# A hybrid RWKV-7 / convolution / expert block: a fourth buffer for split weights, recurrence input begun four steps ahead, one small weight split per pass

## The chip, the cores and the metric

One core of one Trainium2 chip runs the whole program in one launch. The time is device microseconds of one execution; before and after are compared by medians of several runs, and the profile comes from one further execution.

## What is computed

A diffusion-backbone block over 2048 latent tokens and 256 context tokens of width 1024: a modulated RMS norm, one input projection, two branches beside each other (a bidirectional RWKV-7 recurrence over 8 heads of 64, and a gated convolution of width 3), an output projection, then 16 experts that each take their best 256 tokens. Cut to what the change touches:

```python
px = modulate(rmsnorm(x, norm1_g), sh1, sc1) @ w_in            # 1024 -> 1792 + 1536 columns
xr, xk, xv, xw, xa, xgl = split_rwkv(px_rw, shift_mu, grid_shift(px_rw))
def step(s, inp):                                              # the recurrence, both directions
    r_t, w_t, k_t, v_t, a_t, b_t = inp
    sa = einsum('bhvk,bhk->bhv', s, a_t)
    s = s * w_t[:, :, None, :] + sa[..., :, None] * b_t[:, :, None, :] + v_t[..., :, None] * k_t[:, :, None, :]
    return s, einsum('bhvk,bhk->bhv', s, r_t)
g = sigmoid(xgl) @ g_lora_up                                   # "second low-rank weights", 128 x 512
a_x = (groupnorm(y) * gn_g + gn_b + bonus) * g
x = x + g1 * (concat([a_x, short_conv(px_cv, conv_w)]) @ w_out)
out = rmsnorm(x + g2 * expert_choice_ffn(modulate(rmsnorm(x))), final_g)
```

## The kernel before, in words

Large products run in three matmuls instead of one: each operand is cut into a high piece (a cast to fp32r) and a low piece (the rest), and high·high, high·low and low·high are added up in PSUM. `split` (L127 to L134) makes the pieces of a weight: ScalarE casts (L129), then VectorE subtracts (L134). The tiles are `wH` and `wL`, in the pool `sh` that the first half of the program shares, three buffers each.

The program has four stages. First the conditioning (`ada_first`). Then the **projection** (`proj_phase`): four passes over 512 tokens each (pass 0 has the context too), and in each pass a loop over 14 column blocks. A block is `load_block` (two loads `wr` of 256 KB, two splits), then `block_mm` (L262), then an evacuation of PSUM into `e` by ScalarE, then the work on the block before, taken from `queue`: `post_wa`, `post_k` (blocks 1 to 4), `post_r` and `post_kd` (blocks 5 to 8, with the long VectorE scans `ct`, L508), `post_g` (block 9), `post_v` (blocks 10 to 13). `block_mm` goes through the tiles of 256 tokens one after the other, and in each through eight 128-row slices of the weights, the first four from the first half's pieces, the last four from the second half's:

```python
for (hH, hL), ps in zip(tiles, outs):
    for kt in range(KT):
        wH, wL = ws[kt // (KT // 2)]
        for wa, ha in ((wH, hH), (wH, hL), (wL, hH)):
            nc.tensor.matmul(ps, wa[:, kw, :], ha[:, kt, :], ...)
```

So for two tiles a block is 48 matmuls: 12 on the first half, 12 on the second, 12 on the first, 12 on the second. `gupH` and `gupL`, the pieces of the gate's low-rank weights (L324, L338), are made once, before the first pass, and stay.

Third is the **recurrence** (`wkv_phase`), 36 steps of 64 tokens, in both directions at once. For step s, `front(s)` makes masked products `g` (a tile with AHEAD = 5 buffers), `solve(n)` inverts triangles of the two steps 2n and 2n+1 on VectorE with 30 pairs of small instructions (L818, L820), after a trip of `g` through memory (`TI`) and before another one (`TO`), `merge(s)` reads `TO` back into `g` and begins with VectorE's transpose `tz` (L836), and `chain(s)` is the recurrence proper, which ends in the new state `Sb` (L886). `scale(n)` loads and scales the inputs of two steps. `begin(s)` is `front(s)`, and after odd s also `solve(s // 2)`. After `chain(s)` and `ready(s+1)` (the merge) come `scale((s+5) // 2)` if s is odd, `begin(s+5)`, and `fill`, which issues the convolution's products (`conv_gen`, again with `load_block`), the rest of the conditioning and the output projection as filler.

Fourth are the top-256 search and the experts (`moe_phase`, L1429 and L1446), with pools of their own.

The program text gives priorities; a scheduler sets the order of each engine's instructions from them, from the buffers and from its own timeline, and the engines then run that fixed order, each in order. The queue that issues nearly all loads and stores is SP's.

Of the kernel before, what the change touches and what calls it, by code (L numbers as in the profile page):

```python
# [7 lines left out]
F32 = mybir.dt.float32  # L8
# [12 lines left out]
KT = 8  # L21
# [115 lines left out]
def ada_first(ctx, tc, k, I, pool, psum, RH, RL, early):  # L137
# [18 lines left out]
    for kt in range(KT):  # L156
        if kt == 4:
            early(-2)
        for q in range(4):
            wH = k.bp.tile([128, 512], F32R, name="awH", tag="wH", bufs=3)  # L160
            wL = k.bp.tile([128, 512], F32R, name="awL", tag="wL", bufs=3)
            split(k, nc, wH, wL, w[kt][:, q * 512:q * 512 + 512], "act")
            nc.tensor.matmul(ps[q], sp[:, kt], wH, start=kt == 0, stop=False)
            nc.tensor.matmul(ps[q], sp[:, kt], wL, start=False, stop=kt == KT - 1)
# [76 lines left out]
def load_block(tc, k, I, b):  # L241
# [3 lines left out]
    for half in range(2):  # L245
        w = k.bp.tile([128, KT // 2, 128], F32, name="wr", bufs=2)
        nc.sync.dma_start(w, I["w_in"][b][:, half * KT // 2:(half + 1) * KT // 2])
        wH = k.bp.tile([128, KT // 2, 128], F32R, name="wH", bufs=3)
        wL = k.bp.tile([128, KT // 2, 128], F32R, name="wL", bufs=3)
        split(k, nc, wH, wL, w, "act")  # L250
        hs.append((wH, wL))
# [14 lines left out]
def proj_phase(ctx_, tc, k, I, S, fill):  # L266
    nc = tc.nc
    bp = k.bp
    with ExitStack() as ctx:
# [53 lines left out]
        up = pool.tile([128, 2, 2, 512], F32R, name="up", bufs=1)  # L323
        gupH = pool.tile([128, 512], F32R, name="gupH", bufs=1)  # L324
        gupL = pool.tile([128, 512], F32R, name="gupL", bufs=1)
        halo = pool.tile([128, 14, 2, PR], F32, name="halo", bufs=1)
        gn = pool.tile([128, 2, 512], F32, name="gn", bufs=1)

        def small():
            for q, nm in enumerate(("wup2", "aup2")):  # L330
# [4 lines left out]
                nc.vector.tensor_tensor(up[low, q], upr[low], up[low, q].bitcast(F32), op=OP.subtract)  # L335
            gupr = pool.tile([128, 512], F32, name="gupr", tag="sg", bufs=2)
            nc.sync.dma_start(gupr, I["gup"])
            split(k, nc, gupH, gupL, gupr, "act")  # L338
            nc.sync.dma_start(gn, _dap(I["gnrows"], 0, [[0, 128], [512, 2], [1, 512]]))
# [222 lines left out]

        def post_g(units, es):
            for u, e in zip(units, es):
                t0, n, _ = u
# [128 lines left out]
def wkv_phase(ctx_, tc, k, I, S, fill):  # L694
    nc = tc.nc
    with ExitStack() as ctx:
# [26 lines left out]
        NS = NCC + NCL  # L723
        AHEAD = 5
        k.y = {}
# [201 lines left out]
        begin(2)  # L927
        begin(3)
        scale(2)
        fill(1)  # L930
        begin(4)
        ready(0)
        for s in range(NS):
            chain(s)
            ready(s + 1)
            if s % 2:
                scale((s + 5) // 2)
            begin(s + AHEAD)
            fill(75 // 20 + 1 if s < TURN else 100, s >= TURN)
# [49 lines left out]
def conv_out_gen(tc, k, I, S):  # L989
# [5 lines left out]
    for i in OUT_ORDER:  # L995
# [4 lines left out]
        nc.sync.dma_start(cv, _dap(S["CV_"], r0, [[T, 128], [128 * T, 4], [1, 128]]))  # L1000
        aH = bp.tile([128, 4, 128], F32R, name="caH", tag="wH", bufs=3)
        aL = bp.tile([128, 4, 128], F32R, name="caL", tag="wL", bufs=3)
        split(k, nc, aH, aL, cv, "act")
# [9 lines left out]
def out_gen(tc, k, I, S):  # L1013
# [62 lines left out]
    def halves(j, x, y):  # L1076

        pt = turned(j, fl(y), 0)
        aH = bp.tile([128, 4, 128], F32R, name="oaH", tag="wH", bufs=3)
        aL = bp.tile([128, 4, 128], F32R, name="oaL", tag="wL", bufs=3)  # L1080
        split(k, nc, aH, aL, pt, "act")
# [8 lines left out]
    def square(x, ss):  # L1090
        junk = bp.tile([128, x.shape[-1]], BF, name="ojunk", tag="wL", bufs=3)
        nc.scalar.activation(junk, x, AF.Square, accum_out=ss)
# [8 lines left out]
    def flat(j, x, n):  # L1101
        pt = turned(j, x, 512 * n)
        tag = dict(tag="wH", bufs=3) if j < LAST else dict(tag="ev", bufs=5)
        z = bp.tile([128, 4, 128], F32, name="oxt", **tag)
# [553 lines left out]
```

## Time and profile before

| | us |
|---|---|
| median of 3 runs | 3159.18 (3146.18 to 3162.34) |
| the profiled execution | 3142.96 |
| its span, first to last instruction | 3141.1 |
| TensorE (PE) busy | 2881.8 (92%) |
| VectorE (DVE) busy | 2141.5 (68%) |
| ScalarE (ACT) busy | 1385.0 (44%) |
| GpSimd (POOL) busy | 667.4 (21%) |
| mean granted TensorE clock | 0.930 of full |

The conditioning lies in the span's first 50 us, the projection from there to about 626, the recurrence to about 1905, the search to about 1967, the experts to the end. A busy PE is one with matmuls in flight, at whatever clock; "granted clock" is 1.00 at 2.4 GHz and 0.50 at 1.2 GHz, and a mean between them is a mix of both in time. In a row on waits, the engine before the arrow stood idle until the instruction behind the arrow had ended.

### The profile page before, as it was taken

The page shows a single profiled execution, that of the slowest core. Times are in us where ns is not written, and L with a number is a line of the kernel's source. Part 1 is how long each engine was busy: PE and PEld are TensorE (multiplying, and loading weights), DVE is VectorE, ACT ScalarE, POOL GpSimd, SP SyncE. Part 2 cuts the span into 40 slices and gives each one's busy share as a digit, 9 for nine tenths or more (in the row PEclk, how much of TensorE's full clock was granted, in tenths as well). Part 3 has the DMA queues.
Part 4 walks back from the last instruction along what each step waited for, and adds up shares of the span by engine and source line. Part 5 has one row for each costly group of instructions (what it writes and reads, how often), then busy time and mean ns, then how long its engine had stood idle before and what let it go on. Part 6 is the DMA issues. An engine that isn't in the chain of part 4 may idle for free. (4 is left out here: it accounts for less than half of the span.)

```text
span 3141.1 us, 62585 instructions
## 1 busy us (share of the span) xinstructions
PE 2881.8 (92%) x24367; PEld 2612.9 (83%) x24367; DVE 2141.5 (68%) x4611; ACT 1385.0 (44%) x2279; POOL 667.4 (21%) x893
## 2 busy tenths in 40 slices
PE   6988989889999999999999994999999999999997
PEld 4877978878888888778888873998999899999886
DVE  7688687766666666667767646666666666666776
ACT  6556645423344443224445443444444444444453
POOL 0243242533333322112222121000000000000011
PEclk8989999977999999998788986999999999999998
DMA  6466555666666655766665551666666666666886
GB/s 248 144 201 193 178 175 170 201 170 152 154 169 165 173 141 162 204 176 169 164 151 143 124 165 47 201 219 205 188 204 204 195 197 208 207 203 206 267 285 228
DMA packets 408745, 577.43 MB, mean 184 GB/s; under 512 B 175864, under 2 KB 257912, under 8 KB 407424
## 3 DMA queue, kind: packets, MB, share of 16 engines
q1 hardware_dynamic: 397504, 533.58, 56.4%
q0 software_dynamic: 10656, 38.80, 5.3%
q8 instruction: 191, 3.13, 0.4%
q10 hardware_dynamic: 288, 1.05, 0.1%
q14 instruction: 106, 0.87, 0.1%
HBM read 444.73 MB, written 128.59 MB: 183 GB/s over the span
## 5 line engine op out<-in xcount | busy, mean ns | idle before, releaser
L129 ACT CAST wH<-wr 128x1024 fp32r<-128x1024 f32 (+1 forms) x592 | 528.9, 897 | 844.7 <-PE pg L1429 408.8
L134 DVE TENSOR_TENSOR wL<-wr,wH 128x1024 fp32r<-128x1024 f32 (+1 forms) x586 | 627.6, 1076 | 353.5 <-ACT wH L129 347.6
L1429 PE MATMUL pg<-xH,wH 128*128 128x256 f32 x2048 | 585.4, 286 | 15.8 <-ACT s L1433 15.8
L1429 PE MATMUL pg<-xL,wH 128*128 128x256 f32 x2048 | 576.2, 282 | 0.0
L1429 PE MATMUL pg<-xH,wL 128*128 128x256 f32 x2048 | 575.7, 281 | 0.0
L262 PE MATMUL pj<-hH,wH 128*128 128x256 f32 x1600 | 478.0, 299 | 25.5 <-ACT cu L671 7.4
L262 PE MATMUL pj<-hH,wL 128*128 128x256 f32 x1600 | 469.4, 294 | 23.6 <-DVE wL L134 22.6
L262 PE MATMUL pj<-hL,wH 128*128 128x256 f32 x1600 | 468.1, 293 | 1.4 <-DVE hL L134 1.1
L1429 PEld LDWEIGHTS pg<-xH,wH 128*128 128x128 f32 x2048 | 389.5, 190 | 17.9 <-ACT s L1433 16.5
L1429 PEld LDWEIGHTS pg<-xL,wH 128*128 128x128 f32 x2048 | 389.3, 190 | 1.5
L1429 PEld LDWEIGHTS pg<-xH,wL 128*128 128x128 f32 x2048 | 389.5, 190 | 0.0
L262 PEld LDWEIGHTS pj<-hH,wH 128*128 128x128 f32 x1600 | 318.4, 199 | 37.6 <-DVE cu L674 8.4
L262 PEld LDWEIGHTS pj<-hH,wL 128*128 128x128 f32 x1600 | 316.6, 198 | 30.9 <-DVE wL L134 28.9
L262 PEld LDWEIGHTS pj<-hL,wH 128*128 128x128 f32 x1600 | 318.5, 199 | 5.6 <-DVE hL L134 2.0
L1488 POOL DMA_INDIRECT ACC<-o,it x30 | 50.8, 1694 | 954.4 <-DVE o L1474 800.7
L1446 PE MATMUL pd<-wH,hL 128*128 128x512 f32 x512 | 201.9, 394 | 0.0
L1446 PE MATMUL pd<-wL,hH 128*128 128x512 f32 x512 | 201.9, 394 | 0.0
L1446 PE MATMUL pd<-wH,hH 128*128 128x512 f32 x512 | 199.9, 395 | 0.0
L818 DVE TENSOR_TENSOR x<-X,x 128x120 f32<-128x120 f32 (+12 forms) x540 | 157.8, 296 | 57.7 <-DMA X<-TI 46.0
L820 DVE TENSOR_TENSOR X<-X,x 128x120 f32<-128x120 f32 (+12 forms) x540 | 163.0, 305 | 12.3
L782 PE MATMUL pg<-ar,bk 64*128 64x128 f32 x1152 | 141.0, 323 | 17.1 <-DVE g L784 7.5
L782 PEld LDWEIGHTS pg<-ar,bk 64*128 64x128 f32 x1152 | 114.4, 215 | 33.7 <-issue 13.5
(428 smaller groups left out, 5456.9 us busy)
## 6 DMA issues: line engine op xcount, KB each, us to landing
wr<-in_w_gate_dram SPq DMA_DIRECT2D x128, 512.0 KB, 4.2
wr<-in_w_up_dram SPq DMA_DIRECT2D x128, 512.0 KB, 4.8
wr<-in_w_down_dram SPq DMA_DIRECT2D x128, 512.0 KB, 3.3
wr<-in_w_in_dram SPq DMA_DIRECT2D x208, 256.0 KB, 3.2
bk<-KBD SPq DMA_DIRECT2D x36, 512.0 KB, 5.6
ar<-NR SPq DMA_DIRECT2D x36, 512.0 KB, 5.9
adaw<-in_ada_b_dram SPq DMA_DIRECT2D x32, 512.0 KB, 3.7
inc<-C SPq DMA_DIRECT2D x36, 256.0 KB, 3.1
```

The costliest lines, as they stand in the source:

```text
L129: nc.scalar.copy(H_, src)
L134: (leng or nc.vector).tensor_tensor(L_, src, H_.bitcast(F32), op=OP.subtract)
L262: nc.tensor.matmul(ps, wa[:, kw, :], ha[:, kt, :], start=m == 0, stop=m == 3 * KT - 1)
L782: nc.tensor.matmul(pg[:, p], bk[rows, p], ar[rows, p], start=True, stop=True)
L818: nc.vector.tensor_tensor(tv, X[:, 0:r, t:t + 1].to_broadcast([128, r, m]), x[:, t:t + 1, t + 1:].to_broadcast([128, r, m]), op=OP.mult)
L820: nc.vector.tensor_tensor(X[:, 0:r, t + 1:], X[:, 0:r, t + 1:], tv, op=OP.add)
L1429: nc.tensor.matmul(ps, a[:, ws], b[:, kt], start=i == 0, stop=i == 23)
L1446: nc.tensor.matmul(po[2 * m + n], a[:, f, ms], b[:, ns], start=f == 0 and q == 0, stop=f == FB - 1 and q == 2)
L1488: nc.gpsimd.indirect_dma_start(out=S["ACC"], out_offset=bass.IndirectOffsetOnAxis(ap=ids[m][:, :1], axis=0), in_=o, in_offset=None, comput ...
```

## The change

Three edits. All tiles with the tags `wH` and `wL` get four buffers. `gupH` and `gupL` are no longer kept: `post_g` loads and splits the weights in each of the four passes, into a tile that shares the two buffers of `bk` (tag `kd`). In the recurrence AHEAD is 4 (four buffers of `g`), the prologue begins steps 0 to 3 instead of 0 to 4, and `begin(s + AHEAD)` stands before `scale`.

```diff
@@ ada_first, load_block, conv_out_gen, out_gen (all uses of the tags wH and wL)
-        wH = k.bp.tile([128, KT // 2, 128], F32R, name="wH", bufs=3)
-        wL = k.bp.tile([128, KT // 2, 128], F32R, name="wL", bufs=3)
+        wH = k.bp.tile([128, KT // 2, 128], F32R, name="wH", bufs=4)
+        wL = k.bp.tile([128, KT // 2, 128], F32R, name="wL", bufs=4)
@@ proj_phase
-        gupH = pool.tile([128, 512], F32R, name="gupH", bufs=1)
-        gupL = pool.tile([128, 512], F32R, name="gupL", bufs=1)
@@ small()
-            gupr = pool.tile([128, 512], F32, name="gupr", tag="sg", bufs=2)
-            nc.sync.dma_start(gupr, I["gup"])
-            split(k, nc, gupH, gupL, gupr, "act")
@@ post_g(units, es)
+            gupr = pool.tile([128, 512], F32, name="gupr", tag="sg", bufs=2)
+            nc.sync.dma_start(gupr, I["gup"])
+            gup = pool.tile([128, 2, 512], F32R, name="gup", tag="kd", bufs=2)
+            gupH, gupL = gup[:, 0], gup[:, 1]
+            split(k, nc, gupH, gupL, gupr, "act")
             for u, e in zip(units, es):
@@ wkv_phase
-        AHEAD = 5
+        AHEAD = 4
@@
         begin(2)
-        begin(3)
         scale(2)
         fill(1)
-        begin(4)
+        begin(3)
         ready(0)
         for s in range(NS):
             chain(s)
             ready(s + 1)
+            begin(s + AHEAD)
             if s % 2:
                 scale((s + 5) // 2)
-            begin(s + AHEAD)
             fill(75 // 20 + 1 if s < TURN else 100, s >= TURN)
```

Because the scheduler sets the order, instructions move in the first three stages on every engine; in the experts' stage TensorE's order is the same row for row. Two places matter below.

VectorE in the second pass, around blocks 7 and 8. `nrb<-e_3138` and `nrb<-e_3246` mix the results of blocks 7 and 8; `wL_3302` is the second half of block 9's pieces, `wL_3414` the first half of block 10's. Before:

```order
L425 SCALAR_TENSOR_TENSOR nrb_2741<-e_3138,cv_117,nrb_2741 128x8x64
L284 RECIPROCAL ssr_3817<-sss_3815 128x1
L285 TENSOR_SCALAR xt_3796<-xt_3796,ssr_3805 128x1024
L285 TENSOR_SCALAR xt_3808<-xt_3808,ssr_3817 128x1024
L508 SCALAR_TENSOR_TENSOR ct_3263<-rmask_423,sg_3261 128x512
L512 TENSOR_SCALAR bk_3164<-a_3175,cv_117,omka_421 128x8x64
L515 SCALAR_TENSOR_TENSOR bk_3164<-nrb_2741,a_3175 128x8x64
L425 SCALAR_TENSOR_TENSOR nrb_2741<-e_3246,cv_117,nrb_2741 128x8x64
L134 TENSOR_TENSOR wL_3302<-wr_3299,wH_3301 128x512
L508 SCALAR_TENSOR_TENSOR ct_3281<-rmask_423,sg_3279 128x512
L134 TENSOR_TENSOR wL_3414<-wr_3411,wH_3413 128x512
```

With the change (tile numbers are one lower: `e_3137` and `e_3245` are the same blocks' results, `wL_3413` and `wL_3419` the two halves of block 10):

```order
L420 SCALAR_TENSOR_TENSOR nrb_2740<-e_3137,cv_117,nrb_2740 128x8x64
L518 SCALAR_TENSOR_TENSOR kqb_2739<-kqb_2739,cv_117,nrb_2740 128x512
L507 TENSOR_SCALAR bk_3145<-a_3156,cv_117,omka_421 128x8x64
L510 SCALAR_TENSOR_TENSOR bk_3145<-nrb_2740,a_3156 128x8x64
L503 SCALAR_TENSOR_TENSOR ct_3172<-rmask_423,sg_3170 128x512
L134 TENSOR_TENSOR wL_3413<-wr_3410,wH_3412 128x512
L507 TENSOR_SCALAR bk_3163<-a_3174,cv_117,omka_421 128x8x64
L510 SCALAR_TENSOR_TENSOR bk_3163<-nrb_2740,a_3174 128x8x64
L134 TENSOR_TENSOR wL_3419<-wr_3416,wH_3418 128x512
L503 SCALAR_TENSOR_TENSOR ct_3262<-rmask_423,sg_3260 128x512
L420 SCALAR_TENSOR_TENSOR nrb_2740<-e_3245,cv_117,nrb_2740 128x8x64
```

By the mix of block 8 the low pieces of block 10 are now both made; before, the second half of block 9 was still to come.

VectorE in the recurrence, from the last instruction of a solve (here the one of steps 18 and 19) to the transpose that begins the merge of its first step. Before:

```order
L820 TENSOR_TENSOR X_14284<-X_14284,x_14283 128x15
L784 TENSOR_TENSOR g_15022<-pg_15023,mask0_7113 128x512
L1008 TENSOR_TENSOR cx_14427<-pj_14435,cx_14427 128x512
L766 TENSOR_TENSOR bk_15423<-bk_15423,ep_15428 128x8x64
L784 TENSOR_TENSOR g_15022<-pg_15024,mask0_7113 128x512
L784 TENSOR_TENSOR g_15022<-pg_15035,mask1_7119 128x512
L1008 TENSOR_TENSOR cx_14427<-pj_14449,cx_14427 128x512
L134 TENSOR_TENSOR caL_14762<-ccv_14759,caH_14761 128x512
L784 TENSOR_TENSOR g_15022<-pg_15036,mask1_7119 128x512
L766 TENSOR_TENSOR ar_15424<-ar_15424,em_15427 128x8x64
L836 STREAM_TRANSPOSE tz_15365<-g_13900 32x512
```

With the change:

```order
L820 TENSOR_TENSOR X_14600<-X_14600,x_14599 128x15
L766 TENSOR_TENSOR at_15467<-ar_15456,ep_15460 128x512
L1007 TENSOR_TENSOR cx_14381<-pj_14403,cx_14381 128x512
L134 TENSOR_TENSOR caL_14823<-ccv_14820,caH_14822 128x512
L836 STREAM_TRANSPOSE tz_15282<-g_14243 32x512
```

Over the 18 solves, at most six rows stand between the two in 2 of 18 before, and in 15 of 18 with the change. The transpose needs the trip of the solved triangles through `TO`.

## Rows read from the trace of the kernel before

**Rows 1.** Busy time by stretch; its length, engine busy (instructions), granted clock, DMA share, GB/s

```profile
core 0: us, PE busy (x) PEld busy (x) DVE busy (x) ACT busy (x) POOL busy (x), PEclk, DMA share, GB/s
265.00:315.00 50.00, 39.44 (x255) 35.56 (x254) 49.69 (x58) 34.33 (x59) 27.16 (x25) 0.89 0.74 229
315.00:400.00 85.00, 81.09 (x614) 75.31 (x613) 59.77 (x92) 53.25 (x94) 24.86 (x42) 0.98 0.50 165
400.00:445.00 45.00, 34.03 (x224) 31.05 (x224) 43.79 (x47) 16.87 (x28) 31.23 (x25) 0.91 0.72 221
1250.00:1850.00 600.00, 582.36 (x5901) 495.51 (x5900) 394.08 (x1251) 239.44 (x465) 118.57 (x161) 0.91 0.62 158
```

**Rows 2.** TensorE's waits from 50 to 626: us, times, longest

```profile
PE pj L262 <- DVE wL L134: 22.6, 18, 3.6
PE pj L262 <- ACT wH L129: 3.2, 5, 1.4
PE pw L577 <- DVE gt L585: 4.1, 1, 4.1
```

**Rows 3.** TensorE's waits from 265 to 315, then from 400 to 445

```profile
PE pj L262 <- DVE wL L134: 8.2, 3, 3.6
...
PE pj L262 <- DVE wL L134: 8.5, 5, 3.2
```

**Rows 4.** Timeline around 424 to 428: start, us, instruction, [idle before <-what ended it]

```profile
423.84 0.28 PE L262 MATMUL pj<-hH,wH 128*128 128x256 f32 x1
423.96 0.28 PE L262 MATMUL pj<-hL,wH 128*128 128x256 f32 x1
...
425.28 1.59 POOL L514 TENSOR_TENSOR bk<-kqb,bk 128x512 f32<-128x512 f32 x1 [0.42 <-POOL kqb L525]
...
425.67 1.75 DVE L134 TENSOR_TENSOR wL<-wr,wH 128x512 fp32r<-128x512 f32 x1
...
427.47 0.58 PE L262 MATMUL pj<-hH,wL 128*128 128x256 f32 x1 [3.24 <-DVE wL L134]
```

**Rows 5.** The low pieces' subtractions and the casts, 50 to 626 (min/median/max; busy, mean ns)

```profile
L134 DVE TENSOR_TENSOR wL<-wr,wH x123: 659/692/1804, 70.3 to 625.1; 128x512 fp32r<-128x512 f32 x123
...
L129 ACT CAST wH<-wr 128x512 fp32r<-128x512 f32 x124 | 75.6, 617 | 111.2 <-PE pj L262 53.6 <-DMA wr<-in_w_in_dram 53.5 <-PE pc L262 3.8
```

**Rows 6.** The one split of the gate's weights: duration min/median/max, start

```profile
L134 DVE TENSOR_TENSOR gupL<-gupr,gupH x1: 684/684/684, 36.8 to 36.8; 128x512 fp32r<-128x512 f32 x1
```

**Rows 7.** DMA issues of the recurrence: count, KB each, median us to landing

```profile
TO<-X SPq DMA_DIRECT2D x36, 128.0 KB, 3.2
g<-TO SPq DMA_DIRECT2D x72, 64.0 KB, 3.7
```

**Rows 8.** Waits in the recurrence: of VectorE, of ScalarE, of TensorE

```profile
DVE tz L836 <- DMA g<-TO: 13.5, 6, 3.4
...
ACT wH L129 <- PE pj L262: 117.5, 46, 7.5
...
PE pu L869 <- ACT w L863: 12.4, 6, 4.6
```

**Rows 9.** VectorE's timeline, 1613 to 1736: two states, and one solve with its merge

```profile
1614.81 0.85 DVE L886 TENSOR_TENSOR Sb<-sc,pc 64x256 f32<-64x256 f32 x2
...
1646.86 0.19 DVE L818 TENSOR_TENSOR x<-X,x 128x30 f32<-128x30 f32 x1
...
1693.59 0.18 DVE L820 TENSOR_TENSOR X<-X,x 128x15 f32<-128x15 f32 x1
...
1710.11 0.68 DVE L836 STREAM_TRANSPOSE tz<-g 32x512 f32<-32x512 f32 x1
...
1731.81 0.85 DVE L886 TENSOR_TENSOR Sb<-sc,pc 64x256 f32<-64x256 f32 x2
```

**Rows 10.** The state updates from 1250 to 1850 (four rows each step): first and last start

```profile
L886 DVE TENSOR_TENSOR Sb<-sc,pc x80: 405/422/1406, 1261.5 to 1831.1; 64x256 f32<-64x256 f32 x80
```

**Rows 11.** The solves' multiplies in the whole program: duration min/median/max in ns

```profile
L818 DVE TENSOR_TENSOR x<-X,x x540: 146/257/1354, 664.0 to 1792.3; 128x120 f32<-128x120 f32 x37, 128x126 f32<-128x126 f32 x18, 128x78 f32<-128x78 f32 x18, 128x99 f32<-128x99 f32 x17
```

More of the change, by code (lines that the diff above doesn't have):

```diff
@@ L159, in ada_first @@
         for q in range(4):
-            wH = k.bp.tile([128, 512], F32R, name="awH", tag="wH", bufs=3)
-            wL = k.bp.tile([128, 512], F32R, name="awL", tag="wL", bufs=3)
+            wH = k.bp.tile([128, 512], F32R, name="awH", tag="wH", bufs=4)
+            wL = k.bp.tile([128, 512], F32R, name="awL", tag="wL", bufs=4)
             split(k, nc, wH, wL, w[kt][:, q * 512:q * 512 + 512], "act")
@@ L1000, in conv_out_gen @@
         nc.sync.dma_start(cv, _dap(S["CV_"], r0, [[T, 128], [128 * T, 4], [1, 128]]))
-        aH = bp.tile([128, 4, 128], F32R, name="caH", tag="wH", bufs=3)
-        aL = bp.tile([128, 4, 128], F32R, name="caL", tag="wL", bufs=3)
+        aH = bp.tile([128, 4, 128], F32R, name="caH", tag="wH", bufs=4)
+        aL = bp.tile([128, 4, 128], F32R, name="caL", tag="wL", bufs=4)
         split(k, nc, aH, aL, cv, "act")
@@ L1078, in halves @@
         pt = turned(j, fl(y), 0)
-        aH = bp.tile([128, 4, 128], F32R, name="oaH", tag="wH", bufs=3)
-        aL = bp.tile([128, 4, 128], F32R, name="oaL", tag="wL", bufs=3)
+        aH = bp.tile([128, 4, 128], F32R, name="oaH", tag="wH", bufs=4)
+        aL = bp.tile([128, 4, 128], F32R, name="oaL", tag="wL", bufs=4)
         split(k, nc, aH, aL, pt, "act")
@@ L1090, in square @@
     def square(x, ss):
-        junk = bp.tile([128, x.shape[-1]], BF, name="ojunk", tag="wL", bufs=3)
+        junk = bp.tile([128, x.shape[-1]], BF, name="ojunk", tag="wL", bufs=4)
         nc.scalar.activation(junk, x, AF.Square, accum_out=ss)
@@ L1102, in flat @@
         pt = turned(j, x, 512 * n)
-        tag = dict(tag="wH", bufs=3) if j < LAST else dict(tag="ev", bufs=5)
+        tag = dict(tag="wH", bufs=4) if j < LAST else dict(tag="ev", bufs=5)
         z = bp.tile([128, 4, 128], F32, name="oxt", **tag)
```

## The prediction, made before the changed kernel ran

> **What bounds the kernel now.** I read the busy time by stretch first. In the projection TensorE is close to full where VectorE has time to spare (315 to 400: 81.1 of 85 us, VectorE 59.8), and loses a fifth or more of the time where VectorE has none: from 265 to 315 VectorE is busy 49.7 of 50 us and TensorE 39.4, from 400 to 445 it is 43.8 of 45 against 34.0 [rows 1]. These are the blocks of `post_r` and `post_kd`. The list of TensorE's waits names what it stands for there: the low pieces of the weights, 22.6 us in the projection, and the high pieces, 3.2 us [rows 2]; 8.2 and 8.5 us of it lie in the two full stretches [rows 3]. The timeline shows one such wait: matmuls had come every 0.12 us, then TensorE stands 3.24 us until a subtraction ends that itself took 1.75 us, begun while GpSimd worked on `bk` [rows 4]. In the recurrence TensorE is busy 582 of 600 us from 1250 to 1850 [rows 1]: it is the bound there too, though at a granted clock of 0.91. The experts' stage keeps TensorE's order and has pools of its own, so I count nothing there.
>
> **A, the fourth buffer in the projection: -22 us.** With three buffers the second half of a block takes the buffer of the first half of the block before, which is read up to that block's 36th matmul of 48, and is needed after 12 matmuls of its own block: 24 matmuls, at 0.12 us [rows 4] 2.9 us, for a cast of 0.62 us and a subtraction of 0.66 to 1.80 us [rows 5] that both stand in line on their engines. With four it takes the buffer of the block before that: 60 matmuls, 7.2 us; the first half goes from 48 to 60. The order shows that the scheduler uses it: at the mix of block 8, block 10's pieces are made, where block 9's second half was open. The waits are 25.8 us in all [rows 2]. Of them 16.7 us stand in the two full stretches [rows 3]; the other 9.1 us go, since VectorE has room there. In the full stretches a buffer makes no VectorE time; it lets TensorE run ahead, by 7.2 - 2.9 = 4.3 us in each, 8.6 us, and leaves VectorE's arrears to the next stretch, which has 25 us of idle VectorE [rows 1]. I take 13 of the 16.7. Ends: 0 and -25.8. What is late next is VectorE's own work, which delays evacuations.
>
> The Trainium skill (SBUF — State Buffer, "Who interferes with whom") says that a VectorE instruction with two SBUF inputs and a GpSimd instruction that reads SBUF exclude each other for a whole instruction; the 1.75 us beside a minimum of 0.66 agree with it. By that rule an earlier subtraction can meet GpSimd as well as a late one, and A would be the 9.1 us alone: the first rival below.
>
> **B, the clock: -4 us.** The two full stretches have 0.89 and 0.91 where the stretch between them has 0.98 [rows 1]. If shorter waits raised them to 0.98, 95 us would shrink by 95 x (1 - 0.90/0.98) = 7.8 us. Where VectorE is the bound a faster TensorE gives nothing, so I take half. Ends: 0 and -7.8.
>
> **C, the gate's weights in each pass: +4 us.** One split goes from the start, four come: three more loads of 256 KB, casts of 0.62 us and subtractions of 0.68 us alone [rows 5, 6], up to 1.8 us beside GpSimd [rows 5]. They fall behind block 9, at the end of the full stretches, where VectorE's time is TensorE's. 3 x about 1.2 us is 3.6. The load waits in SP's queue for a buffer of `sg`, and behind it wait the stores and weight loads after it; the tile shares `bk`'s two buffers, so the cast waits until a `bk` has been stored. Lower end 0, as the load may be early. Upper end: each pass as long as the longest wait at the gate's matmuls now, 4 x 4.1 = 16 us [rows 2].
>
> **D, four steps ahead instead of five: +8 us.** The first merge of a pair needs the solve, which starts when its odd step's `front` is done. That used to be issued after the chain of four steps earlier, now of three. In 15 of 18 pairs at most six rows stand between the last solve row and the transpose, which needs two landings, 3.2 + 3.7 = 6.9 us [rows 7]. With about 2 us of other rows VectorE stands 5 us for each, 75 us, where it now stands 13.5 [rows 8]: some 60 us more idle VectorE. From 1250 to 1850 TensorE idles 17.6 us against VectorE's 206 [rows 1], one in twelve: 5 us, and 3 us for evacuations queued right behind the transpose. The earlier `scale` order costs nothing by itself: the same loads and products, covered by a full TensorE; without that cover they would stand in VectorE's line before the solve. Lower end 0; a gain is possible only through E. Upper end: the second rival.
>
> **E, ScalarE freed of its waits in the recurrence: -3 us.** ScalarE stands 117.5 us at casts whose buffer TensorE still reads, and TensorE stands 12.4 us for the chain's copy `w` on ScalarE [rows 8]. Other inputs hold up that copy too, so I take a quarter. Ends: 0 and -12.4. The convolution's weight splits have the same wider window, but TensorE's waits there are on evacuations.
>
> **Sum:** -22 - 4 + 4 + 8 - 3 = -17 us. The profiled execution of 3142.96 us would become 3126. It lies 16.2 us under the median of the three runs, 3159.18, to which the measurement will be compared, so I predict 3159.18 - 17 = **3142 us**. Two executions of one program here differ by up to 16 us, so about 0.5% is what can be told from no change.
>
> **Rival 1: VectorE stays the bound in the projection, and the waits change their name.** For it: 49.7 of 50 us busy; no edit takes VectorE work out of these stretches and C adds some. Against: the next stretch has room, and the order already carries the pieces ahead. Then A is 9, B and E nothing: -9 + 4 + 8 = +3, 3162 us.
>
> **Rival 2: the solve becomes the recurrence's bound, slower.** From the state after step 26 (1614.8) to that after step 30 (1731.8) are 117 us [rows 9]. In it the transpose could have come at 1693.8 + 6.9 = 1700.7 and came at 1710.1, so 9.4 us were spare: the tight loop is 107.6 us, 46.9 of them the solve (1646.9 to 1693.8) [rows 7, 9]. Steps come every 569.6 / 19.75 = 28.8 us [rows 10]. Four steps ahead, the loop may take 115 us; three ahead, 86.4. So it decides from a solve of 46.9 - (107.6 - 86.4) = 26 us on. Sixty bare instructions of about 0.257 us take 15.4 us [rows 11], so a solve that VectorE serves first stays below it. Halfway between 26 and 46.9 us the loop is 97 us; with one step more it spans four, (97 + 28.8) / 4 = 31.4 us each, 2.6 us too many in each of 20 steps: +53. With A, B, C, E that is -25 + 53 = +28, 3187 us. At 46.9 us it would be +106. Against it: the order puts filler between the steps, and 24 of the output projection's matmuls after the chain's end where 72 stood, so part of a slower chain comes back at its end.
>
> **Rival 3: the change does not do what it says,** the pieces being made no earlier in time: 3159 us. The order speaks against it.
>
> **How the numbers follow.** The forecast has 0.54, rival 1 0.23, rival 2 0.20, rival 3 0.03. The good ends of A, B and E with C and D at 0 give -46, 3113; with the scatter of the runs I go to 3106. Above, rival 1 with C at its upper end gives -9 + 16 + 8 = +15, 3174; a short way into rival 2 makes it 3178. Rival 2's centre stays out. The forecast's own range is 3113 to 3155. About two thirds of the forecast's chance lie beyond 0.5% (0.37), and 0.06 of rival 1's: faster 0.43. Slower: nearly all of rival 2 and a little of rival 1, 0.20. The rest is 0.37.
>
> **What would show it.** A: TensorE's waits for low and high pieces in the projection fall from 25.8 to about 4 us, the two stretches shorten by 5 to 8 us each, VectorE stays full in them. Rival 1: those waits shrink, and others (on `e`, `gt`, `a`) grow as much. C: waits at the gate's matmuls of 1 us a pass. D: VectorE's wait for `TO` near 75 us, while TensorE's idle time from 1250 to 1850 stays under 30 us; rival 2: TensorE's idle there rises over 50 us and the steps come at over 31 us. The prediction is wrong if the projection's stage does not shorten, or if the recurrence lengthens by more than the projection gains.

## The result, and the profile after

The changed kernel takes 3174.63 us (median of 19 runs, 3158.37 to 3195.62); the kernel before, beside it, 3148.25 (19 runs, 3127.39 to 3162.34). The ratio is 1.0085, 95% interval 1.006 to 1.011: some 26 us slower, where 17 us faster was forecast. The profiled execution took 3174.63 us with a span of 3172.8.

Split at the same events in both traces (50 us, the first masked product, the last matmul of the output projection, the first matmul of the experts), the two executions compare so:

| stage | before, us | after, us | TensorE idle before | after |
|---|---|---|---|---|
| projection | 580.1 | 588.2 | 73.9 | 78.2 |
| recurrence | 1260.1 | 1266.0 | 72.9 | 101.7 |
| search | 63.1 | 70.1 | 45.1 | 54.2 |
| experts | 1187.7 | 1198.5 | 51.1 | 57.0 |

No stage became shorter. The experts' stage has the same order of TensorE in both; over the 15 executions profiled in this study it lies between 1180.9 and 1199.1 us, whatever the kernel, so its 11 us are not put down to the change. In the recurrence too, one execution differs from the next: two kernels below with the changed kernel's own order on TensorE (e6 and e11) needed 1280.4 and 1282.5 us there. What the edits do is therefore read from medians, and from what recurs in many traces.

The busy time by stretch of the changed kernel, with the columns and the stretches of [rows 1] and two more, shows the projection:

```profile
core 0: us, PE busy (x) PEld busy (x) DVE busy (x) ACT busy (x) POOL busy (x), PEclk, DMA share, GB/s
...
130.00:205.00 75.00, 58.66 (x404) 53.97 (x403) 66.29 (x94) 35.90 (x71) 33.10 (x33) 0.91 0.72 219
...
265.00:315.00 50.00, 40.17 (x263) 37.08 (x262) 46.76 (x51) 19.28 (x33) 32.52 (x28) 0.88 0.75 229
315.00:400.00 85.00, 79.80 (x585) 74.36 (x584) 60.40 (x93) 53.12 (x91) 21.03 (x39) 0.95 0.55 176
400.00:445.00 45.00, 36.18 (x242) 33.87 (x241) 40.38 (x44) 17.42 (x30) 27.69 (x25) 0.89 0.71 220
445.00:520.00 75.00, 65.62 (x473) 61.17 (x472) 49.86 (x88) 45.55 (x86) 11.93 (x35) 0.91 0.40 130
...
1250.00:1850.00 600.00, 560.37 (x5626) 474.85 (x5624) 395.31 (x1230) 235.06 (x457) 110.02 (x153) 0.90 0.62 156
```

The same two added stretches of the kernel before:

```profile
130.00:205.00 75.00, 64.54 (x461) 60.14 (x460) 66.25 (x94) 35.75 (x71) 38.41 (x37) 0.96 0.70 206
...
445.00:520.00 75.00, 72.65 (x564) 70.21 (x564) 51.40 (x89) 40.53 (x75) 13.37 (x41) 0.98 0.45 145
```

From 265 to 315 and from 400 to 445, TensorE has gained 0.7 and 2.2 us of busy time: the full stretches stay VectorE's. The loss is where nothing was lost before: from 130 to 205 the clock is 0.91 instead of 0.96 and TensorE is 6 us less busy, from 445 to 520 it is 0.91 instead of 0.98 and 7 us less. These windows are cut by time and do not hold the same work: TensorE's 577th matmul of `pj` starts at 159.2 us where it started at 175.4, and its 673rd, two blocks later, at 208.1 against 210.7. It had run 16 us ahead and lost nearly all of it again. TensorE's waits in the projection, 50 to 626 (us in total, times, longest), answer to [rows 2]:

```profile
PE pj L262 <- DVE wL L134: 7.5, 3, 3.0
PE pj L262 <- ACT e L384: 7.4, 5, 2.5
PE pw L498 <- ACT sg L501: 7.1, 5, 2.2
PE pw L544 <- ACT vt L546: 5.8, 3, 3.5
PE pc L262 <- ACT ec L393: 5.5, 1, 5.5
PE acc L527 <- POOL kqb L520: 5.3, 2, 4.1
```

The wait for the low pieces fell from 22.6 us to 7.5. In its place stand waits for evacuations (`e`, `sg`, `vt`, `ec`) and for GpSimd, which in the list of before are 2.8 us or less each. TensorE's idle time in the stage did not fall: 73.9 to 78.2 us.

In the recurrence, VectorE's waits for the two trips through memory are these (from 626 to 1880, answering to [rows 8]; the first row is the way into a solve, the second the way out):

```profile
DVE x L818 <- DMA X<-TI: 63.5, 16, 10.3
...
DVE tz L836 <- DMA g<-TO: 50.1, 16, 5.8
```

In the kernel before, the way in was:

```profile
DVE x L818 <- DMA X<-TI: 46.0, 13, 6.6
```

The wait of `tz` rose from 13.5 to 50.1 us, and the wait on the way in rose by 17.5 us as well. ScalarE's casts wait somewhat less for their buffers, 96.9 us where it was 117.5:

```profile
ACT wH L129 <- PE pj L262: 96.9, 43, 8.0
```

And the state updates of 1250 to 1850, as in [rows 10]:

```profile
L886 DVE TENSOR_TENSOR Sb<-sc,pc x74: 371/421/835, 1250.1 to 1834.6; 64x256 f32<-64x256 f32 x74
```

These 74 rows span 18.25 steps, so a step takes (1834.6 - 1250.1) / 18.25 = 32.0 us, where it was 28.8. Twenty such steps are 64 us longer, but the stage is only 6 us longer: the changed kernel has step 15's state 15 us earlier (1250.9 against 1265.9), and after the last state, 32 us later, 41 us of the stage are left instead of 59. One pair of steps shows why the later steps are slow. VectorE's timeline of the changed kernel (start, us, instruction, idle before): the last row of step 15's state, the last row of the solve of steps 16 and 17, the transpose that begins step 16's merge, and the first direction's rows of step 16's state.

```profile
1250.08 0.84 DVE L886 TENSOR_TENSOR Sb<-sc,pc 64x256 f32<-64x256 f32 x2
...
1261.05 0.19 DVE L820 TENSOR_TENSOR X<-X,x 128x15 f32<-128x15 f32 x1
...
1269.93 0.70 DVE L836 STREAM_TRANSPOSE tz<-g 32x512 f32<-32x512 f32 x1 [5.05 <-DMA g<-TO]
...
1288.35 0.84 DVE L886 TENSOR_TENSOR Sb<-sc,pc 64x256 f32<-64x256 f32 x2
```

The transpose comes 19 us after the state it should have been ready for, after a wait of 5.05 us for `TO`, and the next state needs 18.4 us more. The same four events in the kernel before, where the solve's end and the transpose come first:

```profile
1207.64 0.17 DVE L820 TENSOR_TENSOR X<-X,x 128x15 f32<-128x15 f32 x1
...
1241.35 0.69 DVE L836 STREAM_TRANSPOSE tz<-g 32x512 f32<-32x512 f32 x1
...
1265.06 0.85 DVE L886 TENSOR_TENSOR Sb<-sc,pc 64x256 f32<-64x256 f32 x2
...
1291.51 0.84 DVE L886 TENSOR_TENSOR Sb<-sc,pc 64x256 f32<-64x256 f32 x2
```

There the transpose was issued 24 us before step 15's state was ready. Taken over the 17 pairs after the first, the transpose of the pair's first step starts on the mean 22 us before the end of the state of the step ahead of it in the kernel before (later than it in 3 pairs), and 1 us after it in the changed kernel (later in 8).

### The profile page after: what moved, and what is told of

It is laid out like the page before. It is cut to its first block, busy times and chain, and to the rows that moved or that the text cites. A ratio compares the mean times of both kernels' runs of the same rounds, so it can differ in the third digit from the quotient of the medians.

```text
span 3172.8 us, 62602 instructions
## 1 busy us (share of the span) xinstructions
PE 2865.1 (90%) x24367; PEld 2601.5 (82%) x24367; DVE 2145.3 (68%) x4614; ACT 1387.0 (44%) x2284; POOL 661.8 (21%) x893
## 5 line engine op out<-in xcount | busy, mean ns | idle before, releaser
L262 PEld LDWEIGHTS pj<-hH,wH 128*128 128x128 f32 x1600 | 315.6, 198 | 48.8 <-DVE cu L674 16.4
L818 DVE TENSOR_TENSOR x<-X,x 128x120 f32<-128x120 f32 (+8 forms) x540 | 167.3, 311 | 79.3 <-DMA X<-TI 63.5
L820 DVE TENSOR_TENSOR X<-X,x 128x120 f32<-128x120 f32 (+8 forms) x540 | 162.6, 302 | 12.1
L782 PE MATMUL pg<-ar,bk 64*128 64x128 f32 x1152 | 121.4, 310 | 13.7 <-DVE g L784 8.3
L782 PEld LDWEIGHTS pg<-ar,bk 64*128 64x128 f32 x1152 | 97.4, 204 | 28.4 <-DVE g L784 8.9
```

The lines of the kernel that those rows point to most:

```text
L262: nc.tensor.matmul(ps, wa[:, kw, :], ha[:, kt, :], start=m == 0, stop=m == 3 * KT - 1)
L782: nc.tensor.matmul(pg[:, p], bk[rows, p], ar[rows, p], start=True, stop=True)
L818: nc.vector.tensor_tensor(tv, X[:, 0:r, t:t + 1].to_broadcast([128, r, m]), x[:, t:t + 1, t + 1:].to_broadcast([128, r, m]), op=OP.mult)
L820: nc.vector.tensor_tensor(X[:, 0:r, t + 1:], X[:, 0:r, t + 1:], tv, op=OP.add)
```

## The experiments

Differences are of medians against the kernel before that ran beside each; A is the fourth buffer, C the split in each pass, D the four steps ahead. The ratio is not formed from these medians, and the two can differ by some 5 us (e8: +0.7 us, and a ratio that makes +6). Stage lengths, idle time and clock come from the one profiled execution of each kernel. It lies within 10 us of the kernel's median but for e1 (24 us below, the fastest of its 12) and e5 (20 us above, the slowest of its 12).

| kernel | what it is | time, us | difference | ratio (95%) | projection, us | its clock | recurrence: length, idle | search |
|---|---|---|---|---|---|---|---|---|
| before | | | | | 580.1 | 0.94 | 1260, 73 | 63.1 |
| after | A C D | 3174.63 | +26.4 | 1.0085 (1.006 to 1.011) | 588.2 | 0.92 | 1266, 102 | 70.1 |
| e1 | C | 3140.5 | -13.0 | 0.996 (0.994 to 0.9979) | 573.4 | 0.94 | 1249, 76 | 61.7 |
| e2 | D | 3176.24 | +22.7 | 1.0075 (1.0048 to 1.0101) | 580.0 | 0.93 | 1284, 124 | 62.7 |
| e3 | C D | 3159.81 | +6.3 | 1.0024 (1.0007 to 1.0041) | 575.2 | 0.95 | 1271, 122 | 62.5 |
| e4 | A C, `sc` 3 | 3159.88 | +6.4 | 1.001 (0.9991 to 1.003) | 593.3 | 0.91 | 1261, 96 | 72.4 |
| e5 | C D, 4 KB unused | 3158.06 | +4.7 | 1.0023 (1.0001 to 1.0044) | 575.4 | 0.94 | 1285, 118 | 69.9 |
| e6 | A C D, `m` moved | 3169.7 | +16.3 | 1.0051 (1.0026 to 1.0077) | 593.1 | 0.92 | 1280, 99 | 62.1 |
| e7 | C D, `begin` first | 3170.32 | +16.9 | 1.0059 (1.0035 to 1.0083) | 573.0 | 0.95 | 1296, 107 | 61.5 |
| e8 | C, `begin` first | 3154.04 | +0.7 | 1.0019 (0.9998 to 1.0039) | 570.7 | 0.95 | 1278, 83 | 61.6 |
| e9 | C, A in the recurrence alone, `sc` 3 | 3131.72 | -18.7 | 0.9947 (0.9916 to 0.9979) | 569.6 | 0.94 | 1244, 82 | 70.7 |
| e10 | C, `sc` 3 | 3127.78 | -22.6 | 0.9918 (0.9891 to 0.9945) | 577.2 | 0.94 | 1245, 75 | 63.3 |
| e11 | A C D, `scale` first (built as after) | 3178.9 | +28.5 | 1.0095 (1.006 to 1.013) | 589.5 | 0.91 | 1283, 106 | 70.2 |
| e12 | C D, longer solve | 3240.47 | +87.4 | 1.029 (1.0251 to 1.033) | 575.0 | 0.94 | 1354, 178 | 61.4 |
| e13 | C, longer solve | 3191.8 | +38.7 | 1.0121 (1.008 to 1.0162) | 571.3 | 0.95 | 1318, 132 | 61.7 |

### The parts alone: e1 to e4

e1 is the diff's edits of `proj_phase`, `small` and `post_g` alone. e2 is its edits of `wkv_phase` alone. e3 is both, so the changed kernel with `bufs=3`. e4 is A and C with the recurrence of before, and

```diff
-                    sc = sb.tile([128, HP, C], F32, name="sc", bufs=4)
+                    sc = sb.tile([128, HP, C], F32, name="sc", bufs=3)
```

since a fourth buffer and five steps do not fit into the memory together. A without C has no room in the projection and was not tried.

> The kernel before with the gate's weights split in each of the four passes, and nothing else (three buffers, five steps ahead). If the sum of the forecast was right for this term: +4 us over the kernel before (0 to +16), the start of the recurrence's first masked products moves from 630 us to about 634. Theory 'lead' (the loss comes from beginning the recurrence's input only four steps ahead): within 5 us of the kernel before. Theory 'projection' (the loss comes from the split in each pass, which gives back what the buffers win): +10 to +20 us, the recurrence begins at 640 or later.

> The kernel before with four steps ahead and the order of begin and scale of the change, and nothing else. Theory 'lead': 15 to 30 us slower than the kernel before, TensorE's idle time in the recurrence up by 20 to 30 us (from 66 us between the first masked product and the last state update). The forecast's term for it: +8 us. Theory 'projection': within 5 us of the kernel before.

> The changed kernel with three buffers of the pieces instead of four, all else as in it. If the fourth buffer gains its 22 us as forecast, this is some 20 us slower than the changed kernel (about +45 us over the kernel before). If it gains nothing, since VectorE is the bound of the two full stretches, it is within 5 us of the changed kernel (+20 to +30 us). If the fourth buffer is itself the loss, it is at the time of the kernel before.

> The fourth buffer and the split in each pass, but five steps ahead and scale ahead of begin as before; the tile sc has three buffers instead of four to make room. Theory 'lead': at or below the kernel before, -20 to +5 us. Theory 'projection': as slow as the changed kernel, +20 to +30 us. The forecast's terms without that for the recurrence give -22 - 4 + 4 - 3 = -25 us.

The terms nearly add up. C is worth -13.0 alone and 6.3 - 22.7 = -16.4 beside D. D is worth +22.7 alone and 6.3 + 13.0 = +19.3 beside C. A, the term from which 22 us of gain were expected, costs 26.4 - 6.3 = +20.1, and beside five steps, e4 against e1, 6.4 + 13.0 = +19.4. By the ratios it is 16 to 19 us. 'Lead' was right on e2's time, though not on TensorE's idle time in the recurrence, which rose by 51 us and not by 20 to 30; it missed e1 (a gain where it had none) and just missed e4; 'projection' was wrong on e1; e3 came out nearest its third reading, that the buffer is itself the loss, which I had thought the least likely.

The table shows where A costs: with four buffers in the projection it takes 588 to 593 us (after, e4, e6, e11), with three and C 570 to 577 (e1, e3, e5, e7 to e10, e12, e13); and the search takes 70 to 72 us in after, e4 and e11.

In the recurrence D's 51 us of idle time did not become 51 us of length: the stage of e2 is 24 us longer than before, since TensorE's busy time fell from 1187 to 1160 us there; e3 against e1 has 46 us more idle time and 21 us more length. By the clock records some 12 us of e2's fall, and 5 of e3's, are time at the lower clock; the rest is open.

### Where the fourth buffer costs: e5, e6, e9, e10

In the built program the pool `sh` ends at byte 89,444 of a partition with three buffers and at 93,540 with four; the experts' pool `m` begins at 90,560 in both. In the changed kernel `oxn`, the tile that the last stores read, reaches to 92,768, into `m`; the first loads' own tiles in `m` begin at 111,488 and touch nothing of `sh`. e5 gives e3 the larger `sh` with no buffer, e6 lifts `m` above the larger `sh`:

```diff
@@ e5, on e3
     k.bp = ctx.enter_context(tc.tile_pool(name="sh", bufs=2))
+    k.bp.tile([128, 1024], F32, name="unused", bufs=1)
@@ e6, on the changed kernel
         sx = ctx.enter_context(tc.tile_pool(name="mx", bufs=2))
+        sx.tile([128, 768], F32, name="unused", bufs=1)
```

> The changed kernel with three buffers (as e3), plus an unused tile of 4 KB in the pool sh, so that every later tile lies where the changed kernel has it, and TensorE's order in the projection stays that of e3. Theory 'place': the fourth buffer's cost in the search stage (70 and 72 us with it, 62 to 63 without) comes from where the experts' pool m begins: with a pool sh that ends above it, the first expert's weight loads are issued after the last store of XN. Then the stage is 70 to 73 us here and the kernel 8 us over e3 (+14 to +18 over the kernel before). Theory 'buffers': the stage stays at 62 to 63, and the time at that of e3 (+5 to +10). Of the projection (575 us in e3, 588 and 593 with four buffers): if places in memory lengthened it, it is at 585 or more here; if the buffers did, by the order they allow, it stays within 3 us of 575 and TensorE's time at 1.2 GHz there under 75 us.

> The changed kernel with an unused tile of 3 KB in the pool mx, which moves the experts' pool m above the end of the pool sh; TensorE's order is the changed kernel's, and the first weight loads stand ahead of the last store of XN again. Theory 'place': the search stage falls from 70 to 62 or 63 us and the time by 6 to 10 us against the changed kernel (+17 to +21 over the kernel before). Theory 'buffers': no change against the changed kernel, +23 to +30.

The search stage confirms 'place' both ways: 69.9 us in e5 and 62.1 in e6. Its rows tell the mechanism. Before: the first loads of the experts' weights (SP's issues, first and last start), and VectorE's narrowing of the candidates in the search (busy, mean ns):

```profile
L1394 SPq DMA_DIRECT2D wr<-in_w_gate_dram x7: 327/365/911, 1855.0 to 1971.2; - x7
...
L1292 DVE SCALAR_TENSOR_TENSOR cand<-n,cand 128x8 f32<-128x8 f32 (+1 forms) x10 | 1.9, 186 | 0.3
```

In the changed kernel, SP's timeline, then GpSimd and VectorE beside each other, then the same group of VectorE:

```profile
1908.55 6.17 SPq L62 DMA_DIRECT2D XN<-oxn  x8
1916.58 0.36 SPq L1393 DMA_DIRECT2D wr<-in_w_gate_dram  x1
...
1921.14 9.25 POOL L134 TENSOR_TENSOR wL<-wr,wH 128x1024 fp32r<-128x1024 f32 x4 [2.43 <-ACT wH L129]
...
1923.62 2.19 DVE L1291 SCALAR_TENSOR_TENSOR cand<-n,cand 128x8 f32<-128x8 f32 x1
...
L1291 DVE SCALAR_TENSOR_TENSOR cand<-n,cand 128x8 f32<-128x8 f32 (+1 forms) x10 | 7.3, 730 | 0.3
```

The first load is issued at 1916.6, behind the last store of `XN`, instead of at 1855.0. So the first pieces are made in the middle of the search: GpSimd subtracts from 1921.1 to 1930.4, and VectorE's small instruction, which takes 0.17 us elsewhere, takes 2.19; three of the ten are like this, and the group's mean is 730 ns instead of 186. That is 5.4 of the stage's 7 us. e5, with three buffers, has the late load and the slow group:

```profile
L1393 SPq DMA_DIRECT2D wr<-in_w_gate_dram x5: 327/328/426, 1922.3 to 1940.8; - x5
...
L1291 DVE SCALAR_TENSOR_TENSOR cand<-n,cand 128x8 f32<-128x8 f32 (+1 forms) x10 | 7.3, 730 | 0.3
```

e6, with four, has neither (its output projection ends at 1923.5, so the load again stands ahead of that):

```profile
L1393 SPq DMA_DIRECT2D wr<-in_w_gate_dram x5: 327/363/890, 1905.1 to 1926.5; - x5
...
L1291 DVE SCALAR_TENSOR_TENSOR cand<-n,cand 128x8 f32<-128x8 f32 (+1 forms) x10 | 1.9, 187 | 0.3
```

On the clock, e6 is 10 us faster than the changed kernel as expected (+16.3 against +26.4), while e5 is not slower than e3 (+4.7 against +6.3; 8 were expected). The orders of TensorE, VectorE and ScalarE are the same in e5 and e3 up to 1875 us, so a new order of the recurrence does not hide the 8 us. The intervals of the two ratios, 5 and 7 us to either side, barely leave room for them. The longer search is certain in both traces; that it costs as much of the whole time is shown by e6 alone.

The projection was not moved by places: e5 has 575.4 us there. The two kernels that differ in it by the fourth buffer and little else are e1 and e4. The whole projection of e1, and TensorE's longest waits for the blocks:

```profile
50.00:623.00 573.00, 499.58 (x3677) 469.58 (x3677) 441.61 (x651) 313.36 (x575) 207.84 (x307) 0.94 0.60 184
...
PE pj L262 <- DVE wL L134: 29.2, 18, 3.2
...
PE pj L262 <- ACT e L384: 3.3, 4, 1.8
```

and of e4:

```profile
50.00:643.00 593.00, 514.95 (x3675) 484.10 (x3673) 439.36 (x650) 316.07 (x578) 200.59 (x308) 0.91 0.58 178
...
PE pj L262 <- ACT e L384: 10.4, 5, 3.0
PE pj L262 <- DVE wL L134: 6.6, 3, 3.0
PE pw L498 <- ACT sg L501: 5.8, 5, 1.8
```

At full clock e1's busy time is 499.58 x 0.94 = 470 us and e4's 514.95 x 0.91 = 469: the same work. Of the 20 us by which e4 is longer, 15 are clock and 5 idle time (73.8 to 78.4 us). By the trace's clock records TensorE is granted 1.2 GHz for 64 us of e1's projection and for 111 of e4's; 54 to 78 us in all the kernels with three buffers, 90 to 111 in the four with four. Why is argued, not shown: with four buffers TensorE runs ahead (its 577th matmul of `pj` starts at 159.0 us in e4, at 171.5 in e1) and then stands before `e`, `sg` and the like until VectorE and ScalarE have caught up (the 673rd starts at 208.5 and 207.1), so that about the same idle time comes in denser places. Of all stretches of 10 us in the projection, begun 1 us apart, 8% to 10% have over 4 us of idle time in the four kernels with four buffers and 4% to 7% in the others, and those with under 0.3 us have become more too (47% to 48%, 36% to 44%). Laid end to end, the stretches with over 4 us do not tell the two apart (9% to 10%, 2% to 11%). The Trainium skill (TensorE: Matmul & The Clock Gate, "A second HAM failure mode: psum-queue depth-cycling") has a kernel whose bursts of matmuls with idle time between them let the clock swing and cost throughput, though the median matmul ran at full speed. This agrees with it in so far as TensorE was at full clock for most of e4's projection and lost by the rest; the page's idle times are short ones, and no run here shows which kind lowers the clock.

e9 gives the fourth buffer to the recurrence alone, and e10 is its control:

```diff
@@ e9, on e1 with three buffers of sc (load_block, conv_out_gen, out_gen)
+def piece(k, tag, shape, dt, name):
+    n = k.turns[tag] = k.turns[tag] + 1
+    if k.wx is not None and n % 4 == 3:
+        return k.wx.tile(shape, dt, name=name, tag=tag + "4", bufs=1)
+    return k.bp.tile(shape, dt, name=name, tag=tag, bufs=3)
-        wH = k.bp.tile([128, KT // 2, 128], F32R, name="wH", bufs=3)
+        wH = piece(k, "wH", [128, KT // 2, 128], F32R, "wH")
...
@@ wkv_phase
-        sb = ctx.enter_context(tc.tile_pool(name="wkv", bufs=2))
+        sb = k.wx = ctx.enter_context(tc.tile_pool(name="wkv", bufs=2))
@@ e10, on e1
-                    sc = sb.tile([128, HP, C], F32, name="sc", bufs=4)
+                    sc = sb.tile([128, HP, C], F32, name="sc", bufs=3)
```

> e1 with a fourth buffer of the pieces in the recurrence's stage alone (a tile of the recurrence's own pool that takes every fourth turn; sc has three buffers to make room): the projection keeps three buffers and its order, and the pool sh its size. If the fourth buffer's loss lies in the projection and the search, as the stages of e4 and of the changed kernel say (+17 and +8 us), and it gains in the recurrence, this is 5 to 15 us faster than e1 (-30 to -15 over the kernel before), with the projection at 571 to 576 us and the search at 62. If the fourth buffer gives nothing in the recurrence it is within 5 us of e1; if the recurrence's part was only a chance of the order, it may be slower than e1.

> e1 with three buffers of sc instead of four and nothing else: the control for e4 and e9. The third earlier tile of sc is read by an instruction that VectorE has behind it, so no wait is added; but the scheduler writes the recurrence in another order. If only waits matter: within 4 us of e1 (-17 to -9 over the kernel before). If mere changes of order move the recurrence, as e7 and e8 suggest, it may lie 5 to 15 us to either side, which is then the spread that any reading of these edits in the recurrence has to allow.

The projection stays at 569.6 us, so the loss there does come from the buffers of the projection. But e9 gains nothing over its control: the recurrences are equal, 1244.3 and 1244.8 us, and e9 is 4 us the slower one. Its search takes 70.7 us, which I had not expected: the added tiles lie in the recurrence's pool, which the output projection then uses to its end, and `m` lies over that pool (the tiles are at 200,416 to 204,512, `m` reaches beyond 205,000). No run here moves them to show it. e10 was meant as a control and is the fastest kernel of the study, 0.8% faster than the kernel before. It is 10 us faster than e1, though the intervals just overlap (0.9891 to 0.9945, 0.994 to 0.9979) and the two ran on different chips. So an order of the recurrence that the scheduler merely wrote otherwise may be worth some 10 us, and no smaller difference there is put down to an edit here. Against e10, which has three buffers of `sc` like it, e4 is 29 us slower, where it is 19 against e1.

### Why four steps cost: e7, e8, e11, e12, e13

```diff
@@ e7, on e3; e8, on e1, with scale first
             chain(s)
+            begin(s + AHEAD)
             ready(s + 1)
-            begin(s + AHEAD)
@@ e11, on the changed kernel
-            begin(s + AHEAD)
             if s % 2:
                 scale((s + 5) // 2)
+            begin(s + AHEAD)
```

> e3 with begin(s + 4) ahead of ready(s + 1) in the text, all else as in e3. Theory 'lead': the solve, begun a merge and two transposes earlier, ends earlier by a few us for each pair, and TensorE's idle time in the recurrence falls from 104 us toward 80: 5 to 15 us faster than e3 (-8 to +3 over the kernel before). If the recurrence loses for another reason (the reordered convolution, or the clock), it stays within 4 us of e3 (+4 to +12).

> e1 (five steps ahead, three buffers, the gate's weights split in each pass) with begin ahead of ready as in e7. Theory 'lead': with five steps ahead the transposes of the first merge come 20 to 40 us before the state they are needed with in the first half, so more lead gives little: within 5 us of e1 (-18 to -8 over the kernel before). If it is the place of begin in the text that matters and not the lead, the gain is as large as in e7.

> The changed kernel with scale ahead of begin, as in the kernel before, and all else as in it (four steps ahead, four buffers). If the number of steps is what costs in the recurrence: within 5 us of the changed kernel (+21 to +31 over the kernel before), TensorE's idle time in the recurrence 85 to 105 us. If the order of the two was the cost: 10 to 20 us faster than the changed kernel.

e11 is as slow as the changed kernel (+28.5 against +26.4), and has to be: the scheduler builds the same program from it, instruction for instruction and address for address. So with four steps the order of `begin` and `scale` in the text changes nothing, D is the number of steps alone (with its buffers of `g` and its prologue), and e11 is the changed kernel measured once more: its recurrence took 1282.5 us against 1266.0, which is what one program's executions can differ by. e7 and e8 missed both readings: 11 and 14 us slower than e3 and e1, at both numbers of steps. As a test of the lead e7 is weak, since the transposes came only 2 us earlier with it (on the mean 0.9 us before the state instead of 0.9 after). TensorE's idle time did fall, from 122 to 107 us, but both recurrences had more time at 1.2 GHz than those they are compared with (290 us against 213, and 291 against 212); what in the order does that I did not find.

e12 and e13 add to each solve, ahead of its way out, on e3 and e1:

```diff
             xf = X.rearrange("p a b -> p (a b)")
+            for _ in range(20):
+                nc.vector.tensor_scalar(xf, xf, 1.0, None, op0=OP.mult)
```

> e3 (four steps ahead, three buffers) with twenty more VectorE instructions at the end of each of the 18 solves, each a multiplication of X by 1.0: they add 20 x about 0.4 us = 8 us to each solve and to VectorE, 144 us in all, and change no value. Theory 'lead': with four steps ahead the first merge's transpose comes after the last state's end in about half of the pairs, so a longer solve is paid for there: 5 us or more in each of 17 pairs, +80 us or more over e3. If the solve is not in the chain (theory 'load': four steps ahead cost through VectorE's order or the clock), the 144 us of VectorE work cost the same here as in e13, within 15 us.

> e1 (five steps ahead, three buffers) with the same twenty instructions in each solve. Theory 'lead': the transposes have 24 us to spare on the mean, so +10 to +40 us over e1, and less than half of what e12 adds to e3. Theory 'load': as much as e12 adds to e3, within 15 us.

The added instruction, in e13 (duration ns min/median/max):

```profile
L823 DVE TENSOR_SCALAR X<-X x360: 369/426/1531, 695.6 to 1855.0; 128x512 f32<-128x512 f32 x180
```

At four steps ahead they cost 87.4 - 6.3 = 81 us, at five 38.7 + 13.0 = 52. The difference of 29 us is twice what 'load' allowed, and e12 meets 'lead'; e13 does not: 52 is over half of 81. Nor does it refute 'load': the four intervals together leave some 20 us to either side of the 29, and in the traces TensorE's idle time in the recurrence rises by the same 55 us in both pairs (122 to 178, 76 to 132). What the transposes show is this. With five steps the longer solve still uses up the lead, 24 us before the state on the mean to 8, and 5 of 17 come too late instead of 1; with four, 1 us after the state becomes 10, and 13 come too late instead of 8. So in about half of the pairs the state waits for the solve at four steps ahead, and in more pairs at either number when the solve is longer. That this lateness is the whole cost of D is argued, not shown. TensorE's list of waits in e2, which is D alone, has the wait for the transpose as its first row, where the kernel before has 1.8 us in 2 waits in the same place (e3 20.1 in 10, the changed kernel 9.9 in 6, e1 with five steps 9.7 in 3):

```profile
PE pm L839 <- DVE tz L836: 21.9, 10, 5.2
```

## Why the prediction was wrong

Both signs by which the prediction called itself wrong came: the projection did not shorten, and the recurrence lengthened. The steps that failed, term by term:

- **A (-22; the fourth buffer as a whole, with B, E and the search, measured +20).** The step that failed is that in the full stretches a buffer "lets TensorE run ahead" and "leaves VectorE's arrears to the next stretch", which was taken for a gain. The waits for the low pieces did go, as forecast (25.8 us to about 4 forecast, to 8.7 measured). But TensorE's total idle time in the projection did not fall (73.9 to 78.2 us, and 73.8 to 78.4 from e1 to e4): the first rival's words, that the waits change their name, fit the list of waits better than the forecast did. The 25 us of idle VectorE in the next stretch were taken for room; TensorE met the evacuations, which are on ScalarE's and VectorE's way as well, and I had counted only the pieces.
- **B (-4; measured about +15 in e4 against e1).** I read the clock of 0.89 to 0.91 as the consequence of the waits for pieces, and took shorter waits for a faster clock. The clock fell with shorter waits and nearly the same sum of idle time; why is open. This term had the wrong sign, and neither end of its range, 0 and -7.8, allowed that. With A it makes the loss of 13 us (after against e3) to 20 us (e4 against e1) in the projection.
- **The search (not in the sum; +7 to +8 in the stage).** "The experts' stage keeps TensorE's order and has pools of its own, so I count nothing there" failed. Its pools lie over those of the stages before; 4 KB more in `sh` made the first weight loads wait for the last store. e5 and e6 show it. The rule that the prediction named for subtractions beside GpSimd (the Trainium skill, SBUF — State Buffer, "Who interferes with whom") holds in this place too, with 2.19 us for 0.17.
- **C (+4; measured -13).** Of this 3 to 10 us are in the projection: 570 to 577 us in nine kernels with it and three buffers, 580.0 and 580.1 without. The wait at the gate's matmuls stayed at 4 us in e1, as before, though it is now for the new split's cast (in the changed kernel 2.7 us in 3 waits), and the three more loads and splits are paid for nowhere that I can see. The rest, in the recurrence, is no larger than what a mere new order gave in e10, and is left open.
- **D (+8; measured +19 to +23).** The mechanism was right in part and its size was off. VectorE's wait for `TO` was put at 75 us and came to 50 (35 in e2); of the 18 solves 14, and not 15, have at most six rows between their end and the transpose. The wait on the way into a solve, which the term left out, rose too (46.0 us to 93.9 in e2). The step that failed is that TensorE idles only "one in twelve" of VectorE's time: TensorE's idle time in the recurrence rose by 51 us in e2, of which the stage kept 24. The 17.6 us of idle TensorE per 206 of VectorE were a mean over steps of which 7 of 10 first transposes came before the state they were needed with, and did not hold where half of them come after it. The words that the earlier `scale` order costs nothing were right: e11 builds the same program.
- **E (-3; measured 0, e9 against e10).** The step that failed is that the fourth buffer frees ScalarE. Its waits for buffers fell from 117.5 us to 96.9 in the changed kernel, but to 103.5 in e2 with three buffers, and not at all in e4 with four and five steps ahead (120.7); e9 has 109.2 against e10's 115.3, and no shorter recurrence.
- **The rivals.** Rival 1 was right on the projection's waits, and rival 2 on what happens in the recurrence: steps at 32.0 us where it asked for over 31, idle time of 39.6 us from 1250 to 1850, between my two marks of 30 and 50. Rival 2's sum of +28 us came near the measured +26 for other reasons: it has -25 for A, B, C and E, which are +7 together with the search, and +53 for D, which is 19 to 23.

## What to carry to other kernels

A wait that goes need not give back its time: ask which engine is late next in the very place to which the released engine runs ahead, and whether TensorE will then stand there at one time instead of in many. A buffer more is also a pool more: look where the pools of later stages begin, since a load can wait for memory of a stage that it has nothing to do with. A lead in steps is to be compared with the length of the loop that uses it, pair by pair, not by a mean of idle time. And an edit of the text can leave the built program as it was, as e11's did; its run then only repeats the other kernel's.

## What the runs showed of the hardware that was not expected

- With nearly the same idle time in the projection, 73.8 us in e1 and 78.4 in e4, TensorE was granted 1.2 GHz for 64 us in the one and for 111 in the other.
- A VectorE instruction on 128x8 numbers took 1.97 to 2.19 us beside GpSimd's subtractions of 2.35 us each, and 0.17 us without: each of the three ended 0.02 us after the subtraction beside it, so the wait was as long as the rest of the other engine's instruction.
- Executions of one program on one core differ by over 1% (3130.67 to 3173.52 us in 30 runs of the kernel before), and the experts' stage alone by 18 us with one order of TensorE, so that differences of some 10 us need medians.
